# A hybrid encoder on one core: rotary tables built in three parts, and new step times in a list scheduler

## The chip, the cores and the metric

The kernel runs on one core of a Trainium2 chip. The metric is the device time of one execution in microseconds, the median of several runs. TensorE (PE in the profile, PEld for its weight loads) does the matmuls and transposes, VectorE (DVE) and ScalarE (ACT) the elementwise work, GpSimd (POOL) part of the weight preparation, one convolution channel block and the rotations, SyncE (SP) issues most of the transfers.

## The reference

Two layers over 512 tokens of width 1024. Each layer has three parts, and each part ends in a layer normalization of 1.414 times the residual plus the part's result.

```python
def layer(x, mem, cos, sin):
    proj = x @ w_in + b_in                       # 256 + 256 + 32 + 2 * 512 columns
    c_q, c_kv, k_r, u = split(proj)
    y_att = mla_group(c_q, c_kv, k_r, cos, sin)  # 8 heads, rms norms, rotary, softmax
    a, g = split(u)
    h = causal_conv31(a * sigmoid(g)) + dw_b     # depthwise, 512 channels
    y_conv = silu(layer_norm(h))
    x = LN1(ALPHA * x + concat(y_att, y_conv) @ w_o)
    x = LN2(ALPHA * x + memory_cross_attention(x, mem))  # 4 heads, 256 memory tokens
    x = LN3(ALPHA * x + (silu(x @ w_g) * (x @ w_up)) @ w_down)
    return x

cos, sin = cos(positions * inv_freq), sin(positions * inv_freq)   # 512 x 16 each
```

All of it is float32. The kernel keeps float32 accuracy on TensorE by splitting each operand into a rounded part and a rest, so that each product is three matmuls (`mm3`, L250 to L252).

## The kernel before, in words

**Weights.** A weight block is fetched into one of three `raw` buffers by SyncE's queue (L266). ScalarE writes its rounded part (`whi`, L314, or L312 with a gain), and GpSimd (L322) or VectorE (L318) the rest (`wlo`). The raw buffer is free for the next fetch when the rest is written.

**The start.** x comes in four tiles of 128 tokens. TensorE transposes each (`transpose_x`, L426), ScalarE writes the rounded part `xTh` (L429), VectorE the rest `xTl` (L432). The projection's blocks 0 to 2 begin on the first 256 tokens between these transposes. All of it is recorded under `issue_order`, which keeps on each engine the order in which it was written.

**The rotary tables** (`rope_tables`, L347 to L404) are sine and cosine of 64 angles on each partition. The positions come by a GpSimd transfer (L349), 61 small VectorE instructions reduce the angles to a turn, in several pieces so that no accuracy is lost, and two ScalarE activations (L400, L404) take the sines. The call is the last of the start. The instructions' order to what follows, the mixer, is not fixed, and so they mix with the mixer's first instructions.

**The mixer** is written as many streams, generators that yield before each step what the step needs: engine, cost in microseconds, buffers taken and given back, events awaited and fired, a rank. `Weave.run` is a list scheduler: it keeps a clock for each engine, takes again and again the step that can start first (by rank among those that start within 0.05 us), adds its cost to its engine's clock, and lets the stream record its instructions. `issue_order` keeps what comes out. So costs (`pe`, `dve`, `act`, `pool`, `dma`, and the numbers at each yield) shape the order of five engines, and nothing else of the program.

The streams: `gates` runs the projection blocks 0 to 7 in pairs; ScalarE adds the bias to one (L655) and takes tanh of half the other (L662, table set of tanh), VectorE multiplies them into `ch` (L664): the gate products, one for each 128 channels. `convolution(m)` begins with a ScalarE instruction into a PSUM bank (L625) and adds 30 taps on VectorE (L628). For the second channel block, `conv_pool` does it with ScalarE (L613, L617) and GpSimd (L619). `latent(t)` makes the low-rank columns (L702 and around, sums at L708), `queries`, `keys`, `values` and `item_steps` are the attention: scores, maximum (L847), exponential (L852), reciprocal (L855), division (L858), transposes (L863), mixing. `memory_kv` fetches the 256 memory tokens (L544), transposes them (L549), and makes keys and values of the cross-attention. `conv_out` transposes the convolution's result (L911), normalizes and transposes back (L925). `output_half` is the first half of the output projection.

Behind each mixer follow its second half and LN1 (`tail`), the cross-attention and the feed-forward part. They are written out by hand and have no costs.

Of the kernel before, what the change touches and what calls it, by code (L numbers as in the profile page):

```python
# [10 lines left out]
I32 = mybir.dt.int32  # L11
# [6 lines left out]
P = 128  # L18
# [3 lines left out]
NT = SEQ // P  # L22
# [110 lines left out]
def step(eng, cost, get=(), put=(), wait=(), fire=None, lag=0.0, rank=None):  # L133
    return eng, cost, get, put, wait, fire, lag, rank


def pe(n, width, m=P, **kw):
    return step("PE", n * max(width * 0.4219, 0.833 * m) * 1e-3, **kw)


def dve(width, n=1, fixed=70, **kw):
    return step("DVE", n * (width * 1.0417 + fixed) * 1e-3, **kw)


def act(width, n=1, fixed=150, **kw):
    return step("ACT", n * (width * 0.833 + fixed) * 1e-3, **kw)
# [29 lines left out]
def encoder(ctx: ExitStack, tc: tile.TileContext, x_in, mem_in, pos_in, wu, wc, wuq, wukv, wo,  # L176
            xq, xk, xv, xo, fin, fdn, vec, row, out):
    nc = tc.nc

    const = ctx.enter_context(tc.tile_pool(name="const", bufs=1))  # L180
# [146 lines left out]


    ident = const.tile([P, P], F32, name="ident")
    make_identity(nc, ident)  # L330
# [16 lines left out]
    def rope_tables():  # L347
        posi = const.tile([P, NT], I32, name="posi")
        nc.gpsimd.dma_start(out=posi, in_=pos_in)  # L349
        posf = const.tile([P, NT], F32, name="posf")  # L350
# [4 lines left out]
        def t64():  # L355
            return work[:, next(used), :]
# [13 lines left out]
        def whole(dst, src):  # L370
            nc.vector.tensor_copy(n, src)
            nc.vector.tensor_copy(m, n)
            nc.vector.tensor_tensor(dst, src, m, op=ALU.subtract)
# [3 lines left out]
        for src, i in ((al, 4), (ahf, 4), (al, 3), (al, 2), (ahf, 3)):  # L377
            nc.vector.scalar_tensor_tensor(out=tiny, in0=src, scalar=TURN_PARTS[i], in1=tiny,
                                           op0=ALU.mult, op1=ALU.add)
        tot = t64()  # L380
        for first, (src, i) in enumerate(((ahf, 0), (al, 0), (ahf, 1), (al, 1), (ahf, 2))):
            nc.vector.tensor_scalar(pr, src, TURN_PARTS[i], None, op0=ALU.mult)
            if first == 0:
                whole(tot, pr)
            else:
                whole(pr, pr)
                nc.vector.tensor_tensor(tot, tot, pr, op=ALU.add)
                whole(tot, tot)
# [14 lines left out]
        nc.vector.tensor_scalar(a2, a2, 0.25, None, op0=ALU.add)  # L403
        nc.scalar.activation(cosT.rearrange("p t f -> p (t f)"), a2, AF.Sin, scale=TWO_PI)  # L404


# [182 lines left out]
    def mixer(l, xT, blocks, x_src):  # L589
# [100 lines left out]
        def latent(t):  # L690
# [14 lines left out]
            for half in range(2):  # L705
                cs = blk(half, 272)
                yield dve(272, put=("ps",))
                nc.vector.tensor_tensor(c[:, cs], o[half][:, :272], cbias[:, cs], op=ALU.add)  # L708
            yield act(256, 2, get=("scr",), put=("scr",))
            ss = sm(2, "ss")  # L710
# [122 lines left out]
        def item_steps(n_item, pair, t, hs):  # L833
            nk = (t + 1) * P
# [8 lines left out]
            for i, par in enumerate(hs):  # L843
# [4 lines left out]
                                    op=ALU.max, negate=True)  # L848
            yield act(nk, n, put=("ps",))
            p = scr(name="p")  # L850
            for i in range(n):
                nc.scalar.activation(p[:, blk(i, nk)], sp[:, blk(i, nk)], AF.Exp, bias=mx[:, i:i + 1],  # L852
                                     accum_out=su[:, i:i + 1])
            yield dve(1)
            nc.vector.reciprocal(ri[:, :n], su[:, :n])  # L855
            yield step("DVE", n * (nk * 0.52 + 70) * 1e-3)
            for i in range(n):
# [279 lines left out]
    xT = new_xT()  # L1137
    with issue_order(tc, ORDERED):
        for t in range(2):
            transpose_x(x[t], t, xT)  # L1140
        blocks[0].first(xT)
        blocks[1].load()
        transpose_x(x[2], 2, xT)
        blocks[1].first(xT)
        blocks[2].load()
        transpose_x(x[3], 3, xT)
        blocks[2].first(xT)
        rope_tables()
    for l in range(DEPTH):
# [74 lines left out]
```

## Time and profile before

| | |
|---|---|
| median of 3 runs | 1494.85 us (1491.54 to 1496.07) |
| the profiled execution | 1493.32 us, span 1491.4 us |
| granted TensorE clock, mean | 0.994 |
| busy share: PE, PEld, DVE, ACT, POOL | 97%, 84%, 47%, 48%, 31% |
| chain that ended last | PE 75%, DVE 12%, ACT 5%, DMA 4%, POOL 3% |
| read from device memory | 213 MB |

A row of the timeline gives the start, the length, the engine, the line, what it writes and reads, and in brackets how long the engine had been idle before it and what released it. Matmuls overlap, and a row's length holds the drain at its end, so the cost of one in a row of many is the distance of two starts.

### The profile page before, as it was taken

Reading aid. Unit: us, or ns where it says so; the run is one execution under the profiler, and the core shown is the slowest. Engines: PE = TensorE matmul, PEld = TensorE weight load, DVE = VectorE, ACT = ScalarE, POOL = GpSimd, SP = SyncE. Lnnn points to the kernel's source line nnn. Section 1 sums busy time; section 2 is a strip of 40 time slices with the busy share of each in tenths; the row PEclk is TensorE's granted clock in tenths of the full one; section 3 lists DMA queues with packets and bytes.
Section 4 is the critical chain, followed back from the end, with each engine's and each line's share of the span. In section 5 each row is a group of like instructions: output and inputs, shape, how many; then the busy total and the mean of one; then the engine's idle time right before and its main releaser. Section 6 shows DMA issues by size and latency. Waiting matters only on the chain.

```text
span 1491.4 us, 21169 instructions
## 1 busy us (share of the span) xinstructions
PE 1453.1 (97%) x8152; PEld 1256.3 (84%) x8152; DVE 707.6 (47%) x1187; ACT 721.8 (48%) x1278; POOL 466.8 (31%) x665
## 2 busy tenths in 40 slices
PE   8799999999999999999999999999999999999997
PEld 7699988987988888888889999888889888888886
DVE  6999677665511111220469886685663111114005
ACT  3667773453544444553146777624525444446430
POOL 2679771000311111111148877410012111111111
PEclk9899999999999999999999999999999999999999
DMA  5325444242598888998433444423419888889871
GB/s 179 127 70 171 114 128 156 78 161 73 141 223 193 193 196 192 221 201 193 118 116 122 130 127 127 156 71 100 156 48 236 196 190 194 194 193 219 196 140 57
DMA packets 64452, 227.27 MB, mean 152 GB/s; under 512 B 7328, under 2 KB 7360, under 8 KB 64352
## 3 DMA queue, kind: packets, MB, share of 16 engines
q1 hardware_dynamic: 43616, 150.75, 31.1%
q0 software_dynamic: 20736, 75.17, 27.8%
q8 instruction: 64, 1.05, 0.3%
q14 instruction: 36, 0.29, 0.1%
HBM read 213.31 MB, written 8.39 MB: 149 GB/s over the span
## 4 chain that ended last, share of the span: by engine, by line
PE 75%; DVE 12%; ACT 5%; DMA 4%; POOL 3%; issue 1%; SPq 0%; POOLq 0%; DVEq 0%; ACTq 0%
PE accb L250 18%; PE accb L251 18%; PE accb L252 18%; PE psb L250 5%; PE psb L251 5%; PE psb L252 5%; DVE convb L628 3%; DMA raw<-in_xo 3%; DVE wlo L226 1%; DVE p L858 1%; DMA raw<-in_xq 1%; ACT whi L225 1%; PE convb L250 1%; PE convb L252 1%; PE convb L251 1%
## 5 line engine op out<-in xcount | busy, mean ns | idle before, releaser
L250 PE MATMUL accb<-xTh,whi 128*128 128x512 f32 (+1 forms) x1104 | 400.6, 365 | 1.5 <-ACT whi L225 1.3
L251 PE MATMUL accb<-xTl,whi 128*128 128x512 f32 (+1 forms) x1104 | 401.0, 364 | 0.5 <-DVE xTl L432 0.5
L252 PE MATMUL accb<-xTh,wlo 128*128 128x512 f32 (+1 forms) x1104 | 400.3, 363 | 0.1
L287 ACT CAST whi<-raw 128x1024 fp32r<-128x1024 f32 x126 | 132.7, 1055 | 339.4 <-PE accb L251 255.6
L250 PEld LDWEIGHTS accb<-xTh,whi 128*128 128x128 f32 x1104 | 208.7, 190 | 35.7 <-ACT xTh L429 2.7
L251 PEld LDWEIGHTS accb<-xTl,whi 128*128 128x128 f32 x1104 | 209.9, 190 | 32.9 <-DVE xTl L432 1.7
L252 PEld LDWEIGHTS accb<-xTh,wlo 128*128 128x128 f32 x1104 | 209.7, 190 | 32.5 <-DVE wlo L226 0.4
L289 POOL DMA_DIRECT2D wlo<-in_fin x82 | 71.0, 866 | 345.9 <-ACT wlo L288 336.6
L322 POOL TENSOR_TENSOR wlo<-raw,whi 128x1024 fp32r<-128x1024 f32 (+1 forms) x63 | 152.3, 2420 | 62.1 <-ACT whi L314 61.9
L1098 DVE SCALAR_TENSOR_TENSOR scr<-scr,accb 128x512 f32<-128x512 f32 x44 | 30.3, 688 | 253.4 <-ACT scr L1097 253.4
L628 DVE SCALAR_TENSOR_TENSOR convb<-ch,hvec,convb 128x511 f32<-128x511 f32 (+9 forms) x180 | 132.3, 735 | 5.2 <-ACT convb L625 1.7
L288 ACT ACTIVATE wlo<-whi 128x1024 fp32r<-128x1024 f32 x126 | 133.2, 1057 | 2.2
L226 DVE TENSOR_TENSOR wlo<-raw,whi 128x1024 fp32r<-128x1024 f32 (+1 forms) x49 | 56.5, 1158 | 127.2 <-ACT whi L225 126.4
L446 POOL TENSOR_SCALAR ve<-mv 128x1 f32<-128x1 f32 x32 | 27.5, 859 | 244.5 <-DVE mv L467 235.4
L289 POOL DMA_DIRECT2D wlo<-in_fdn x44 | 38.0, 863 | 198.4 <-ACT wlo L288 193.1
L1100 DVE SCALAR_TENSOR_TENSOR hid<-scr,accb 128x512 f32<-128x512 f32 x44 | 30.2, 687 | 136.7 <-PE accb L252 136.7
L225 ACT CAST whi<-raw 128x1024 fp32r<-128x1024 f32 (+1 forms) x49 | 48.9, 1002 | 84.9 <-PE accb L252 33.3
L619 POOL TENSOR_TENSOR cs<-cs,scr 128x511 f32<-128x511 f32 (+29 forms) x60 | 71.5, 1191 | 35.7 <-ACT scr L617 34.5
L314 ACT CAST whi<-raw 128x1024 fp32r<-128x1024 f32 (+1 forms) x63 | 66.7, 1060 | 4.6 <-PE accb L252 1.7
L250 PE MATMUL accb<-whi,hs 128*128 128x512 f32 x176 | 68.6, 390 | 0.0
L251 PE MATMUL accb<-wlo,hs 128*128 128x512 f32 x176 | 68.5, 389 | 0.0
L252 PE MATMUL accb<-whi,hs 128*128 128x512 f32 x176 | 68.5, 389 | 0.0
(295 smaller groups left out, 3165.8 us busy)
## 6 DMA issues: line engine op xcount, KB each, us to landing
raw<-in_fin SPq DMA_DIRECT2D x88, 512.0 KB, 3.6
wlo<-in_fin POOLq DMA_DIRECT2D x82, 512.0 KB, 5.6
raw<-in_fdn SPq DMA_DIRECT2D x44, 512.0 KB, 4.1
wlo<-in_fdn POOLq DMA_DIRECT2D x44, 512.0 KB, 5.9
raw<-in_xk SPq DMA_DIRECT2D x16, 512.0 KB, 3.6
raw<-in_xv SPq DMA_DIRECT2D x16, 512.0 KB, 3.6
raw<-in_wo SPq DMA_DIRECT2D x16, 512.0 KB, 3.6
raw<-in_xq SPq DMA_DIRECT2D x16, 512.0 KB, 3.6
```

Of the source, the lines that this page charges most:

```text
L225: nc.scalar.copy(hi, src)
L226: nc.vector.tensor_tensor(lo, src, hi.bitcast(F32), op=ALU.subtract)
L250: nc.tensor.matmul(o, l[0], r[0], start=first, stop=False)
L251: nc.tensor.matmul(o, l[0], r[1], start=False, stop=False)
L252: nc.tensor.matmul(o, l[1], r[0], start=False, stop=last)
L287: nc.scalar.copy(hi[:, :1024], raw[:, :1024])
L288: nc.scalar.activation(lo[:, :1024], hi[:, :1024].bitcast(F32), AF.Copy, scale=-1.0)
L289: nc.gpsimd.dma_start(out=lo[:, :1024], in_=src, accum_op=ALU.add)
L314: nc.scalar.copy(hi, raw)
L322: eng.tensor_tensor(lo, raw, hi.bitcast(F32), op=ALU.subtract)
L619: nc.gpsimd.tensor_tensor(o[:, d:], o[:, d:], part, op=ALU.add)
L628: nc.vector.scalar_tensor_tensor(out=o[:, d:], in0=src[:, :SEQ - d], scalar=tap(m, d), in1=o[:, d:], op0=ALU.mult, op1=ALU.add)
```

## The change

The positions are fetched at the very start, in front of the identity. `rope_tables` becomes a generator with three stops: part one (up to the small remainder, 13 VectorE instructions) is recorded behind the load of weight block 1, part two (4 instructions) behind that of block 2, part three (the rest, 44 instructions and the two sines) at the end as before. Seven transposes of the identity are recorded in front of everything on TensorE; their result is not read, and since they take a PSUM buffer, the buffers of the next transposes shift by one. And the scheduler's costs change: a matmul costs 0.4167 ns for each column and 0.105 ns for each stationary column, the squares of the rms norm 50 ns more each, an exponential 100 ns more, a reciprocal 120 ns more, and the division counts 1.04 ns instead of 0.52 for each element.

```diff
 def pe(n, width, m=P, **kw):
-    return step("PE", n * max(width * 0.4219, 0.833 * m) * 1e-3, **kw)
+    return step("PE", n * max(width * 0.4167 + 0.105 * m, 0.85 * m) * 1e-3, **kw)
...
+    posi = const.tile([P, NT], I32, name="posi")
+    nc.gpsimd.dma_start(out=posi, in_=pos_in)
     ident = const.tile([P, P], F32, name="ident")
     make_identity(nc, ident)
...
     def rope_tables():
-        posi = const.tile([P, NT], I32, name="posi")
-        nc.gpsimd.dma_start(out=posi, in_=pos_in)
+
         posf = const.tile([P, NT], F32, name="posf")
...
             nc.vector.scalar_tensor_tensor(out=tiny, in0=src, scalar=TURN_PARTS[i], in1=tiny,
                                            op0=ALU.mult, op1=ALU.add)
+        yield
         tot = t64()
...
             if first == 0:
                 whole(tot, pr)
+                yield
...
         nc.scalar.activation(cosT.rearrange("p t f -> p (t f)"), a2, AF.Sin, scale=TWO_PI)
+        yield
...
-            yield act(256, 2, get=("scr",), put=("scr",))
+            yield act(256, 2, fixed=200, get=("scr",), put=("scr",))
...
-            yield act(nk, n, put=("ps",))
+            yield act(nk, n, fixed=250, put=("ps",))
...
-            yield dve(1)
+            yield dve(1, fixed=190)
             nc.vector.reciprocal(ri[:, :n], su[:, :n])
-            yield step("DVE", n * (nk * 0.52 + 70) * 1e-3)
+            yield dve(nk, n, fixed=70)
...
     with issue_order(tc, ORDERED):
+        started = psb()
+        for _ in range(7):
+            nc.tensor.transpose(started[:, 0:P], ident, ident)
         for t in range(2):
             transpose_x(x[t], t, xT)
         blocks[0].first(xT)
         blocks[1].load()
+        rope = rope_tables()
+        next(rope)
         transpose_x(x[2], 2, xT)
         blocks[1].first(xT)
         blocks[2].load()
+        next(rope)
         transpose_x(x[3], 3, xT)
         blocks[2].first(xT)
-        rope_tables()
+        next(rope)
```

What it does to the order is shown at three places. Lines of the changed kernel are four higher in the mixer (L436 is the `xTl` of L432, L632 the tap of L628). First VectorE in the start, from the rest of weight blocks 0 and 1 on; `ropew` is the rotary tables' working tile. Before:

```order
L226 TENSOR_TENSOR wlo<-raw,whi 128x512 x4
L432 TENSOR_TENSOR xTl<-psb,xTh 128x2x128 x4
L226 TENSOR_TENSOR wlo<-raw,whi 128x512 x2
L432 TENSOR_TENSOR xTl<-psb,xTh 128x2x128 x2
L432 TENSOR_TENSOR xTl<-convb,xTh 128x2x128 x2
L351 CAST posf<-posi 128x4
```

Now, from the last instructions of part one on:

```order
L379 SCALAR_TENSOR_TENSOR ropew<-ah,ropew 128x64
L436 TENSOR_TENSOR xTl<-psb,xTh 128x2x128 x4
L226 TENSOR_TENSOR wlo<-raw,whi 128x512 x2
L384 TENSOR_SCALAR ropew<-ah 128x64
L372 CAST ropew<-ropew 128x64
L373 CAST ropew<-ropew 128x64
L374 TENSOR_TENSOR ropew<-ropew 128x64
L436 TENSOR_TENSOR xTl<-convb,xTh 128x2x128 x2
L436 TENSOR_TENSOR xTl<-psb,xTh 128x2x128 x2
L384 TENSOR_SCALAR ropew<-ropew 128x64
```

Thirteen rotary instructions now stand before the third tile's `xTl`, four before the last tile's; behind these the first gate product has 38 in front of it, where all 40 stood in one row before.

The second place is ScalarE from the start of the first convolution to the fifth weight cast of the mixer. Before:

```order
L625 ACTIVATE convb<-ch,vec,hvec 128x512
L655 ACTIVATE scr<-accb,vec 128x512
L314 CAST whi<-raw 128x1024 x2
L662 ACTIVATE scr<-accb,hvec 128x512
L613 ACTIVATE cs_406<-ch,vec,hvec 128x512
L617 ACTIVATE scr<-ch,hvec 128x511
L400 ACT_TABLE_LOAD
L400 ACTIVATE sinT<-ropew 128x64
L314 CAST whi<-raw 128x1024
```

Now:

```order
L629 ACTIVATE convb<-ch,vec,hvec 128x512
L403 ACT_TABLE_LOAD
L403 ACTIVATE sinT<-ropew 128x64
L407 ACTIVATE cosT<-ropew 128x64
L659 ACTIVATE scr<-accb,vec 128x512
L314 CAST whi<-raw 128x1024 x2
L666 ACT_TABLE_LOAD
L666 ACTIVATE scr<-accb,hvec 128x512
L617 ACTIVATE cs_414<-ch,vec,hvec 128x512
L314 CAST whi<-raw 128x1024
```

Both sines and both table loads moved in front of the second tanh, and nothing but the pooled convolution's start is left between it and the cast. In VectorE's order the second gate product stood behind nine taps with rotary instructions between them, and now stands behind ten taps with none between.

The third place is GpSimd in the second layer, up to the last tap of its convolution (128x482) and what comes behind it. Before:

```order
L619 TENSOR_TENSOR cs_7251<-cs_7251,scr 128x485
L322 TENSOR_TENSOR wlo<-raw,whi 128x1024
L805 TENSOR_TENSOR qra<-qs,cosT 128x2x16 x2
L805 TENSOR_TENSOR qrb<-qs,sinT 128x2x16 x2
L808 TENSOR_TENSOR qs<-qra,qrb 128x2x16
L809 TENSOR_TENSOR qs<-qra,qrb 128x2x16
L322 TENSOR_TENSOR wlo<-raw,whi 128x1024
L619 TENSOR_TENSOR cs_7251<-cs_7251,scr 128x484
L619 TENSOR_TENSOR cs_7251<-cs_7251,scr 128x483
L322 TENSOR_TENSOR wlo<-raw,whi 128x1024
L793 COPY qs<-maskp 128x64
L619 TENSOR_TENSOR cs_7251<-cs_7251,scr 128x482
```

Now:

```order
L623 TENSOR_TENSOR cs_7259<-cs_7259,scr 128x485
L322 TENSOR_TENSOR wlo<-raw,whi 128x1024
L623 TENSOR_TENSOR cs_7259<-cs_7259,scr 128x484
L623 TENSOR_TENSOR cs_7259<-cs_7259,scr 128x483
L623 TENSOR_TENSOR cs_7259<-cs_7259,scr 128x482
L797 COPY qs<-maskp 128x64
L809 TENSOR_TENSOR qra<-qs,cosT 128x2x16 x2
L809 TENSOR_TENSOR qrb<-qs,sinT 128x2x16 x2
```

Three weight subtractions and two query rotations that stood before the last tap stand behind it. On TensorE the transposes of the convolution's result moved with it, in front of some 140 matmuls, 96 of them of the memory keys.

## Rows read from the trace of the kernel before

**Rows 1.** The page, busy us and share of each engine

```profile
PE 1453.1 (97%) x8152; PEld 1256.3 (84%) x8152; DVE 707.6 (47%) x1187; ACT 721.8 (48%) x1278; POOL 466.8 (31%) x665
```

**Rows 2.** Stretches of the mixers: length, busy PE, PEld, DVE, ACT, POOL, clock, DMA

```profile
65.00:228.00 163.00, 157.39 (x1265) 147.11 (x1264) 133.76 (x241) 120.75 (x298) 125.87 (x202) 1.00 0.42 128
745.00:975.00 230.00, 223.66 (x1652) 204.59 (x1651) 179.79 (x314) 149.45 (x351) 155.67 (x223) 0.99 0.39 126
```

**Rows 3.** TensorE's wait for the memory tokens: timeline, and a stretch at half clock

```profile
60.65 1.11 PE L549 MATMUL psb<-ident,mem 128*128 128x128 f32 x4 [8.93 <-DMA mem<-in_mem]
...
54.30:64.60 10.30, 3.95 (x12) 3.28 (x13) 9.98 (x12) 7.60 (x11) 9.94 (x7) 0.50 0.50 167
```

**Rows 4.** Timeline of SyncE's queue, 41 to 57 us

```profile
41.52 14.44 SPq L266 DMA_DIRECT2D raw<-in_wc  x3
56.01 0.43 SPq L544 DMA_DIRECT2D mem<-in_mem  x1
```

**Rows 5.** Timeline of GpSimd, the weight subtraction at 53 us

```profile
53.26 2.35 POOL L322 TENSOR_TENSOR wlo<-raw,whi 128x1024 fp32r<-128x1024 f32 x1 [1.21 <-ACT whi L314]
```

**Rows 6.** Timeline of ScalarE, 49 to 60 us

```profile
49.25 0.82 ACT L613 ACTIVATE cs<-ch,vec,hvec 128x512 f32<-128x512 f32 x1 [8.70 <-DVE ch L664]
...
52.16 1.03 ACT L314 CAST whi<-raw 128x1024 fp32r<-128x1024 f32 x1
...
57.46 1.08 ACT L314 CAST whi<-raw 128x1088 fp32r<-128x1088 f32 x1
58.56 1.28 ACT L662 ACT_TABLE_LOAD   x1
59.85 0.69 ACT L662 ACTIVATE scr<-accb,hvec 128x512 f32<-128x512 f32 x1
```

**Rows 7.** Timeline of VectorE, 17 to 63 us

```profile
17.67 1.42 DVE L432 TENSOR_TENSOR xTl<-psb,xTh 128x256 fp32r<-128x256 f32 x4 [3.09 <-ACT xTh L429]
...
21.41 0.76 DVE L432 TENSOR_TENSOR xTl<-psb,xTh 128x256 fp32r<-128x256 f32 x2 [1.13 <-ACT xTh L429]
...
22.75 0.16 DVE L351 CAST posf<-posi 128x4 f32<-128x4 int32 x1
...
26.41 0.20 DVE L382 TENSOR_SCALAR ropew<-ropew 128x64 f32<-128x64 f32 x1
...
28.68 2.42 DVE L372 CAST ropew<-ropew 128x64 f32<-128x64 int32 x1
...
35.97 0.68 DVE L664 SCALAR_TENSOR_TENSOR ch<-scr 128x512 f32<-128x512 f32 x1
...
48.53 0.68 DVE L664 SCALAR_TENSOR_TENSOR ch<-scr 128x512 f32<-128x512 f32 x1
...
53.45 2.20 DVE L403 TENSOR_SCALAR ropew<-ropew 128x64 f32<-128x64 f32 x1
55.58 7.67 DVE L628 SCALAR_TENSOR_TENSOR convb<-ch,hvec,convb 128x498 f32<-128x498 f32 x10
```

**Rows 8.** Timeline of TensorE at the start

```profile
7.80 1.12 PE L426 MATMUL convb<-ident,x 128*128 128x128 f32 x4 [1.11 <-DMA x<-in_x]
```

**Rows 9.** Waits of TensorE in layer 1: timeline, and waits from 80 to 230 us

```profile
77.16 0.66 PE L549 MATMUL psb<-ident,mem 128*128 128x128 f32 x4 [1.13 <-DVE mTl L243]
...
PE psb L863 <- DVE p L858: 2.3, 5, 0.9
```

**Rows 10.** Layer 2: waits of TensorE, last tap of GpSimd, first transpose of the convolution

```profile
PE psb L863 <- DVE p L858: 2.5, 4, 1.0
...
905.36 1.04 POOL L619 TENSOR_TENSOR cs<-cs,scr 128x482 f32<-128x482 f32 x1 [1.16 <-ACT scr L617]
...
909.44 0.29 PE L911 MATMUL psb<-ident,ch 128*128 128x128 f32 x1
```

**Rows 11.** Timeline of TensorE, two matmuls of 256 columns

```profile
24.69 0.28 PE L251 MATMUL accb<-xTl,whi 128*128 128x256 f32 x1
24.81 0.29 PE L252 MATMUL accb<-xTh,wlo 128*128 128x256 f32 x1
```

## The prediction

> **What bounds the kernel now.** I read the page first, then the stretches of the stages, then the waits and the timeline of each engine in the one stretch where TensorE stands still. On the page TensorE is busy for 1453.1 us, 97% of the span, so only its idle time, its half-clock time and its order can give anything back [rows 1]. The profiled execution took 1493.32 us, 1.5 us less than the median of 1494.85; the sums below are made against 1493.3. In the two mixers TensorE is busy 157.4 of 163 us and 223.7 of 230 us [rows 2], so some 12 us of idle time lie there, in many small pieces; the diff reaches nothing behind the mixers.
>
> One piece is large. TensorE stops after the first half of projection block 6 at about 51.7 us and waits 8.93 us for the memory tokens, till 60.65; its clock falls to the lower level, 1.2 GHz, at about 54.3 and is back at 64.6, so that about 4 us of work run at half speed, another 2 us lost [rows 3].
>
> Why are the memory tokens late? Their transfer is issued only at 56.01, behind three weight transfers that had held SyncE's queue since 41.52 [rows 4]; it lands 4.6 us later. The last of the three needs a raw buffer, which comes free when GpSimd's subtraction that began at 53.26 ends, 2.35 us on [rows 5]. That subtraction follows ScalarE's cast at 52.16, which stood behind the start of the pooled convolution at 49.25, which had waited 8.70 us for VectorE's gate product [rows 6]. VectorE made that product only at 48.53: the first product came at 35.97 behind 40 rotary instructions, and between the two stand nine taps and most of the remaining rotary chain [rows 7]. Rotary instructions of 64 columns take 2.2 to 2.4 us instead of 0.2 (28.68, 53.45) where GpSimd subtracts at the same time (from 53.26 on) [rows 5, 7]. A chain of 0.2 us instructions on VectorE sets when TensorE gets its memory tokens.
>
> **The change, part by part.** *Rotary tables, parts one and two.* Thirteen and four instructions, 3.66 us from 22.75 to 26.41, move in front of the two waits of VectorE that end at 17.67 (3.09 us idle) and 21.41 (1.13 us idle) [rows 7]: 2.7 us fit into the first, 0.9 into the second. Cost nothing; without that cover they would delay the casts of x by at most the same 3.7 us.
>
> *Part three and the first product.* The order now puts 38 rotary instructions before the first product instead of the 23 that were left: 15 more of 0.23 us (ten in 26.41 to 28.68 [rows 7]), 3.4 us. The two long ones among them remain. First product: 35.97 - 3.66 + 3.4 = 35.7. Nothing gained yet.
>
> *The second product.* Behind the first now come 0.6 us of product, the six last rotary instructions (1.3 us) and ten taps, 7.67 us for ten [rows 7], with no rotary work between them: 35.7 + 0.6 + 1.3 + 7.7 = 45.3, not 48.53. ScalarE must have the gate's tanh by then. Its order now has, after the first product, convolution start (0.8), table load (1.28), two sines (0.5), the gate's bias step (0.7), two casts (2.0), table load (1.28), tanh (0.7), load and cast by their rows [rows 6]: from 36.4, 7.2 us, 43.6. That is 1.7 us early. Here a rule speaks against the change, since both loads now stand in front of the second product. The trace shows a load beginning 0.02 us after the cast before it (57.46 + 1.08) and the tanh 0.01 us after its end [rows 6], so nothing beside 1.28. The Trainium skill (ScalarE: Activation LUTs, "What ACT_TABLE_LOAD costs") puts a drain of 1.38 us beside each load. By that, the two drains would make the tanh end at 46.4, the memory term below 1.1 us smaller and the sum 1486.2; this case's trace does not show the drain, and I go by the row.
>
> *The memory transfer.* Between second product and cast there now stand only the product and the pooled start: 1.4 us, where 3.63 us stood with the load and sine. Cast at 46.7 instead of 52.16: 5.4 us earlier. Subtraction, last weight transfer and memory transfer follow at the same distances: issue at 50.6, landing at 55.2. TensorE's order up to that point is the same. **Gain 5.4 us.** Bounds: 0, if something else holds the transfer; 8.9 plus 2.0, the wait and the half clock. The idle time left, 51.7 to 55.2, is longer than the 2.6 us after which the clock fell, so I leave the 2 us where they are.
>
> *Warm-up transposes and the earlier table of positions.* Seven transposes of the identity, 0.28 us each at the start (1.12 us for four [rows 8]), 2.0 us, run before x arrives or in the 1.11 us wait for x at 7.80. GpSimd issues the positions' transfer first, which puts the identity 0.8 us later. A sooner clock or a later start of up to 3 us ends in the wait at 51.7 us. Nothing.
>
> *VectorE's lead in layer 1.* The four rotary instructions stretched under GpSimd from 39 to 55.6 us (the last: 2.20 instead of 0.2 [rows 7]) go, and 3.7 us went into idle time, so VectorE is some 10 us ahead. The wait for it at 77.16, 1.13 us, should go, and of the softmax waits of layer 1, 2.3 us [rows 9], about half, since the scheduler now counts 0.1 us more for an exponential, 0.12 for a reciprocal and 0.27 for a division over 512. **Gain 2.2 us**, bounds 0 and 3.4; a new order may also cost as much as these waits amount to.
>
> *The new order in layer 2.* No rotary work is there; only step times move things. A 512-column matmul counts 0.227 instead of 0.216 us, which tells the scheduler that VectorE, ScalarE and GpSimd have more time for each of TensorE's steps. Half of the softmax waits there, 2.5 us [rows 10], against somewhat tighter convolution ends (next part): **gain 0.6 us**, bounds -5 and 5 (2.5 with further small ones and the half clock behind one of them).
>
> Sum: 5.4 + 2.2 + 0.6 = 8.2; 1493.3 - 8.2 = **1485.1 us**, 0.55% below. The median may stand up to 1.5 us higher.
>
> **The rivals.** *The convolutions' transposes come too early (slower).* In layer 2 the transposes of the convolution's output begin at 909.44 [rows 10]. Some 140 matmuls that stood in front of them now stand behind: 96 of 256 columns, 11.5 us at 0.12 us from start to start [rows 11], and small ones, about 15 us in all. GpSimd's last tap ended at 906.40, 3.0 us before they began [rows 10]. On GpSimd three weight subtractions of 2.4 us and two rotations, some 2 us each, moved behind that last tap, 11 us. If GpSimd keeps its pace, the last tap ends near 895, and TensorE arrives near 894: a wait of a microsecond. But that tap had itself waited 1.16 us for ScalarE. If ScalarE sets the pace instead and the tap stays at 906, the wait is 12 us plus 2 us of half clock, and in layer 1, where the same transposes moved up by 5.5 us, some 6 more: 1493.3 - 8.2 + 20 = 1505. It decides above 13 us of such waits together. Against it: the scheduler saw ScalarE's steps too, and about a dozen of ScalarE's instructions moved behind the tap as well. Chance 0.09.
>
> *The memory wait stays.* If the tanh, not the taps, is last, or the transfer is held by another buffer, the chain gains under 2 us and the rest is the scatter of a new order: 1491. For it: all of the 5.4 us rests on one chain of six waits. Chance 0.19.
>
> *The wait shrinks below what drops the clock.* If TensorE comes later to the wait and the tokens earlier, both by a microsecond, the 2 us of half clock go, and with both layers' softmax waits at their bounds the time is 1479. Chance 0.12.
>
> **How the numbers follow.** The main case has 0.60, with its own range 1481 to 1490. Range over the cases: 1478 to 1494, which leaves out the slower rival and the lowest corner of the third. About 0.3%, 4.5 us, is what a measurement of this kernel can tell from no change; against 1494.85 faster means under 1490.4 and slower above 1499.3. Faster: 0.12 and most of the main case, 0.56, makes 0.68. Same: 0.19 plus the main case's edge, 0.23. Slower: 0.09.
>
> **What would show it.** Right: the second gate product near 45 us, its ScalarE successor and the weight cast near 47, the memory transfer issued near 50.6, TensorE's wait 3 to 4.5 us instead of 8.9; no VectorE instruction of 64 columns at 2 us after 38 us; no wait at the second pair of memory transposes. Wrong: a wait of 8 us or more there still; ScalarE's tanh ending after the tenth tap; a wait above 2 us before the convolution transposes of either layer, with GpSimd's last tap as its releaser; a stretch of half clock in the mixers longer than before.

## The result, and the profile after

The changed kernel takes 1513.07 us (median of 5 runs, 1511.20 to 1514.83), the kernel before 1491.54 us in the same comparison (5 runs, 1488.17 to 1496.07): a ratio of 1.0143, 95% interval 1.0122 to 1.0165. That is slower by 1.4%, where 0.55% faster was forecast, and outside the range.

The page of the changed kernel, span and busy times, against [rows 1]:

```profile
span 1511.1 us, 21192 instructions
PE 1460.3 (97%) x8159; PEld 1261.0 (83%) x8159; DVE 702.5 (46%) x1187; ACT 722.3 (48%) x1278; POOL 469.0 (31%) x665
```

The span grew by 19.7 us, and TensorE's busy time by 7.2 us although it does only seven transposes more, about 2 us [rows 8]: part of its work ran at half clock (a stretch of it is shown below); the rest of the 7.2 us was not taken apart. I cut the span at two kinds of TensorE's rows: the transposes of the rotated keys, `kx`, in the mixer (one row a layer) and the last matmul of the output projection's second half (`psb<-whi,yc`).

The timeline of the kernel before, TensorE, `kx` and last `yc` of layers 1 and 2:

```profile
108.61 0.60 PE L748 MATMUL psb<-ident,kx 128*128 128x128 f32 x4
...
266.57 0.39 PE L252 MATMUL psb<-whi,yc 128*128 128x512 f32 x1
...
837.86 0.60 PE L748 MATMUL psb<-ident,kx 128*128 128x128 f32 x4
...
998.14 0.39 PE L252 MATMUL psb<-whi,yc 128*128 128x512 f32 x1
```

The same of the changed kernel:

```profile
103.05 0.60 PE L752 MATMUL psb<-ident,kx 128*128 128x128 f32 x4
...
271.71 0.39 PE L252 MATMUL psb<-whi,yc 128*128 128x512 f32 x1
...
846.14 0.60 PE L752 MATMUL psb<-ident,kx 128*128 128x128 f32 x4
...
1018.77 0.39 PE L252 MATMUL psb<-whi,yc 128*128 128x512 f32 x1
```

Up to the first `kx` the change is 5.6 us ahead. From `kx` to the last `yc` layer 1 takes 168.7 us for 158.0 (266.6 to 108.6 before), layer 2 172.6 for 160.3 (837.9 to 998.1 before); between the two it loses another 3.1 us, at the start of layer 2, where TensorE's waits for GpSimd and VectorE add up to 3.4 us for 0.6 before; and behind layer 2's mixer it gains 1.0. So -5.6 + 10.7 + 3.1 + 12.3 - 1.0 = 19.5 of the 19.7 us. **The start gained about what was forecast; the two mixers lost 26 us, where my worst bounds for a new order were 5 us in layer 2 and 3.4 us in layer 1.**

Where in the mixers? Busy time by stretch (length, PE, PEld, DVE, ACT, POOL, clock, DMA), two stretches that hold most of the two mixers. Before:

```profile
95.00:280.00 185.00, 180.73 (x1362) 164.96 (x1361) 145.07 (x262) 120.35 (x298) 116.52 (x187) 1.00 0.41 126
840.00:1030.00 190.00, 184.12 (x1361) 166.84 (x1360) 141.05 (x249) 112.18 (x272) 99.23 (x148) 0.99 0.40 126
```

The changed kernel, with a short stretch at half clock:

```profile
95.00:280.00 185.00, 173.72 (x1279) 157.32 (x1278) 134.75 (x246) 113.00 (x282) 110.48 (x176) 0.98 0.40 124
840.00:1030.00 190.00, 174.79 (x1288) 157.67 (x1287) 134.53 (x238) 110.66 (x275) 107.81 (x172) 0.99 0.39 122
...
186.90:193.00 6.10, 6.03 (x27) 5.99 (x28) 3.25 (x7) 3.74 (x12) 5.38 (x13) 0.51 0.24 61
```

TensorE stands 16.3 us longer in these 375 us, and no other engine is busier in layer 1 (in layer 2 only GpSimd is, 107.8 of 190 us for 99.2), so no engine became the bound: all of them wait more for each other. In the short stretch behind the longest wait the granted clock is 0.51, that is the lower of its two levels, 1.2 GHz, and TensorE runs 27 matmuls; in the kernel before the same 6.1 us, with another mix of matmuls at full clock, hold 53.

The waits of TensorE in the changed kernel from 95 to 280 us and from 840 to 1030 us (total, times, longest), the larger rows:

```profile
PE accb L816 <- POOL qs L813: 3.8, 2, 2.9
PE psb L867 <- DVE p L862: 2.3, 3, 1.3
PE accb L250 <- DVE qTl L245: 1.6, 1, 1.6
...
PE psb L867 <- DVE p L862: 3.5, 5, 1.0
PE accb L251 <- DVE pl L243: 3.5, 4, 2.1
PE accb L250 <- ACT st L586: 1.9, 2, 1.7
```

All rows of these two answers add up to 25.8 us, the same answers of before to 9.6. The added 16 us have eight or more releasers on three engines; no single wait is it. The longest one, 2.94 us, shows how such a wait can come about; the others were not followed. Timelines of ScalarE, GpSimd and TensorE of the changed kernel, 174 to 187 us:

```profile
174.26 0.46 ACT L934 ACTIVATE scr<-psb,hvec 128x128 f32<-128x128 f32 x1 [0.66 <-PE psb L929]
...
180.09 0.56 ACT L936 ACTIVATE scr<-psb,hvec 128x128 f32<-128x128 f32 x1
180.43 1.15 ACT L314 CAST whi<-raw 128x1024 fp32r<-128x1024 f32 x1
...
181.65 2.38 POOL L322 TENSOR_TENSOR wlo<-raw,whi 128x1024 fp32r<-128x1024 f32 x1 [5.43 <-ACT whi L314]
...
184.59 1.70 POOL L809 TENSOR_TENSOR qrb<-qs,sinT 128x32 f32<-128x32 f32 x2
...
186.58 0.33 POOL L813 TENSOR_TENSOR qs<-qra,qrb 128x32 f32<-128x32 f32 x1
...
186.97 0.69 PE L816 MATMUL accb<-ident,qs 128*128 128x128 f32 x2 [2.94 <-POOL qs L813]
```

The new order puts two tiles of the convolution's output one behind the other. Their 16 activations stand on ScalarE 0.35 us apart, where the scheduler counts 0.257; the weight cast behind them comes at 180.43, GpSimd has been idle for 5.43 us, does the subtraction and only then the rotation for which TensorE has been waiting. By these two figures the 16 activations take 1.4 us more than the scheduler counts, so their cost alone is not the whole of the wait.

### The profile page after: what moved, and what is told of

Same layout as the page of the kernel before. It is cut to its first block, busy times and chain, and to the rows that moved or that the text cites. A ratio compares the mean times of both kernels' runs of the same rounds, so it can differ in the third digit from the quotient of the medians.

```text
span 1511.1 us, 21192 instructions
## 1 busy us (share of the span) xinstructions
PE 1460.3 (97%) x8159; PEld 1261.0 (83%) x8159; DVE 702.5 (46%) x1187; ACT 722.3 (48%) x1278; POOL 469.0 (31%) x665
## 4 chain that ended last, share of the span: by engine, by line
PE 73%; DVE 10%; ACT 6%; DMA 5%; issue 3%; POOL 3%; SPq 0%; POOLq 0%; DVEq 0%; ACTq 0%
PE accb L250 18%; PE accb L251 18%; PE accb L252 18%; PE psb L252 5%; PE psb L250 5%; PE psb L251 5%; DVE convb L632 3%; DMA raw<-in_xo 3%; POOL wlo L322 1%; DVE wlo L226 1%; DVE p L862 1%; PE convb L250 1%; ACT whi L225 1%; PE convb L251 1%; PE convb L252 1%
## 5 line engine op out<-in xcount | busy, mean ns | idle before, releaser
L632 DVE SCALAR_TENSOR_TENSOR convb<-ch,hvec,convb 128x511 f32<-128x511 f32 (+9 forms) x180 | 132.6, 737 | 11.0 <-ACT convb L629 6.6
```

Source lines behind the costliest of these rows:

```text
L632: nc.vector.scalar_tensor_tensor(out=o[:, d:], in0=src[:, :SEQ - d], scalar=tap(m, d), in1=o[:, d:], op0=ALU.mult, op1=ALU.add)
```

## The experiments

Eighteen kernels, each against the kernel before on the same chip; the kernel before had medians of 1490.3 to 1491.5 us, so the medians of the table can be compared with each other to about a microsecond. "Stretches" are `kx` to last `yc` in layers 1 and 2 (158.0 and 160.3 before, 168.7 and 172.6 after).

| kernel | median us | ratio, 95% | stretches |
|---|---|---|---|
| tables_only | 1483.29 | 0.9947 [0.9930, 0.9964] | 157.7, 159.0 |
| pe_cost_only | 1510.69 | 1.0136 [1.0117, 1.0155] | 171.0, 162.1 |
| soft_cost_only | 1501.38 | 1.0071 [1.0056, 1.0086] | 168.1, 160.5 |
| costs_only | 1518.70 | 1.0188 [1.0171, 1.0205] | 169.0, 172.5 |
| pe_up_half | 1499.79 | 1.0061 [1.0044, 1.0078] | 167.8, 162.1 |
| pe_down_half | 1497.91 | 1.0056 [1.0039, 1.0073] | 163.7, 164.5 |
| hop_up | 1500.53 | 1.0063 [1.0046, 1.0080] | 167.8, 168.4 |
| pe_down_7 | 1501.94 | 1.0079 [1.0064, 1.0094] | 169.8, 168.5 |
| all_up_8 | 1501.58 | 1.0077 [1.0062, 1.0092] | 165.1, 169.2 |
| after_hop | 1511.53 | 1.0149 [1.0133, 1.0164] | 166.6, 172.9 |
| after_pe_down | 1508.93 | 1.0140 [1.0120, 1.0160] | 178.9, 160.8 |
| calib_act | 1509.79 | 1.0122 [1.0107, 1.0137] | 169.2, 165.1 |
| calibrated | 1493.76 | 1.0022 [1.0011, 1.0032] | 156.8, 169.2 |
| calib_hop | 1488.15 | 0.9988 [0.9977, 1.0000] | 163.9, 160.4 |
| calib_pe_down | 1490.34 | 1.0002 [0.9993, 1.0012] | 167.3, 160.5 |
| no_warmup | 1484.60 | 0.9960 [0.9946, 0.9975] | 158.1, 158.9 |
| mem_early | 1484.12 | 0.9959 [0.9944, 0.9974] | 157.8, 159.1 |
| mem_both_early | 1484.99 | 0.9955 [0.9939, 0.9972] | 157.7, 159.3 |

**The two halves of the change.** *tables_only* is the changed kernel with the old step times, *costs_only* the kernel before with the new ones; *pe_cost_only* and *soft_cost_only* put in one part of these.

```diff
 # costs_only = both hunks, pe_cost_only = the first, soft_cost_only = the others
-    return step("PE", n * max(width * 0.4219, 0.833 * m) * 1e-3, **kw)
+    return step("PE", n * max(width * 0.4167 + 0.105 * m, 0.85 * m) * 1e-3, **kw)
...
+            yield act(256, 2, fixed=200, get=("scr",), put=("scr",))
...
+            yield act(nk, n, fixed=250, put=("ps",))
...
+            yield dve(1, fixed=190)
...
+            yield dve(nk, n, fixed=70)
```

> The rotary tables in three parts and the warm-up transposes, with all step times of the scheduler as before. If the loss comes from the step times (both theories below), the 6 us that the memory wait gave back stay: 1484 to 1487 us, ratio 0.995 to 0.997. Rival: the three parts cost something behind the memory wait as well; then 1493 us or more.

> The kernel before, with the new cost of a matmul alone. Theory R (ratio): TensorE's cost was too low by about the share by which those of the other engines are too low; raised alone it makes the scheduler count on VectorE, ScalarE and GpSimd being done sooner than they are. Then this edit alone carries the loss: 1508 to 1520 us. Theory S (softmax): the longer softmax steps move the transposes and with them the fill work; then this one stays within 4 us of 1491.5.

> The kernel before, with the new costs of squares, exponentials, reciprocals and divisions alone. Theory R: within 4 us of 1491.5, or somewhat faster, since these costs give the other engines more room. Theory S: it carries the loss, 1508 to 1520 us.

> The kernel before, with all new step times and none of the other edits. If the edits add up, the changed kernel's 1513 plus the 6 us of the memory wait: 1517 to 1521 us under R and S alike. If the tables' new place is part of the loss, under 1510 us.

The tables gain 7.2 us (1490.5 to 1483.3, just below the range expected). The step times lose 28.2 us alone. Their sum, 21.0, is close to the measured 21.5. The order says the same: counted in the traces (tiles by name, buffer numbers left out), TensorE's order of *tables_only* is that of the kernel before, and that of *costs_only* is that of the changed kernel, but for the seven transposes and 16 places, all in the first 21 us. Each part of the step times loses by itself, the matmuls' 20 us, in theory R's range, and the softmax's 11 us, which neither theory had. Whether that is due to these numbers or to any other numbers, these runs do not tell; the next group asks it. Undoing the step times and keeping the tables gives the fastest kernel of this study (with *no_warmup* and the two *mem* kernels, which lie within 1.7 us of it).

**Neighbours of the old step times.** Do the new numbers lose, or would any numbers? In *tables_only* the matmul's number goes up or down by half a per cent or down by 7%, or the price of a hand-over between engines goes from 0.15 to 0.16 us; *all_up_8* takes the new matmul numbers and multiplies the steps of the other three engines by 1.08.

```diff
-    return step("PE", n * max(width * 0.4219, 0.833 * m) * 1e-3, **kw)
+    return step("PE", n * max(width * 0.4240, 0.837 * m) * 1e-3, **kw)   # pe_up_half
+    return step("PE", n * max(width * 0.4198, 0.829 * m) * 1e-3, **kw)   # pe_down_half
+    return step("PE", n * max(width * 0.3924, 0.775 * m) * 1e-3, **kw)   # pe_down_7
...
-    HOP = 0.15
+    HOP = 0.16                                                           # hop_up
...
-    return step("DVE", n * (width * 1.0417 + fixed) * 1e-3, **kw)
+    return step("DVE", n * (width * 1.0417 + fixed) * 1.08e-3, **kw)     # all_up_8; ACT, POOL alike
```

> The tables-only kernel (1483.3 us), with a matmul's cost raised by 0.5% and nothing else. Theory R (what counts is TensorE's cost against that of the other engines): half a percent is a tenth of the new cost's 5 to 11%, so within 2 us: 1481 to 1486. Theory N (any other numbers give another order, and the order before was a chosen one): 5 us or more above, 1488 to 1505 us, since half of the order changes already.

> The tables-only kernel, with a matmul's cost lowered by 0.5%. Theory R: within 2 us of 1483.3, or slightly faster. Theory N: 1488 to 1505 us, as for the raise.

> The tables-only kernel, with a matmul's cost lowered by 7%, the new cost's step in the other direction. Theory R: the other engines get more room; 1475 to 1486 us, not slower. Theory N: 1488 to 1505 us.

> The tables-only kernel, with the new cost of a matmul and 8% more on every step of VectorE, ScalarE and GpSimd, so that the ratio between the engines is the old one. Theory R: the loss of the new matmul cost (20 us) goes: 1480 to 1488 us. Theory N: another order, 1488 to 1508 us, no better than the new matmul cost alone beyond chance.

> The rotary tables alone, with the scheduler's price of a hand-over between engines 0.16 instead of 0.15 us and all step times as they were. No engine's ratio to another changes. Theory N (the old order is a good one among many, and any other number breaks it): 1488 to 1505 us. Theory that it is the step times of particular engines that matter: at most 1486 us.

Five times 1498 to 1502, theory N's range each time; the other theory's ranges, none of them above 1488, were missed each time. Half a per cent on one number, in either direction, puts another instruction in 1,777 or 1,975 of TensorE's 8,159 places, all in the two mixers, and costs 15 to 17 us; the new step times do so in 1,921. So the old order, 1483.3 with the tables, is far better than what its own numbers give next door, and the usual price of leaving it is some 16 us of the 30 that the new step times cost. By this measure the softmax's 11 us is no more than any other numbers cost, and the matmuls' 20 us little more. The two largest of TensorE's waits of *hop_up* from 95 to 280 us:

```profile
PE accb L251 <- DVE pl L243: 3.6, 3, 1.7
PE psb L867 <- DVE p L862: 2.7, 4, 1.1
```

*all_up_8* shows the same from the other side: with all engines' steps raised, the loss is 11 us smaller than the changed kernel's, and no smaller than a neighbour's. *pe_down_7*, the step in the other direction, is no better than a neighbour either. In *hop_up* the waits are again many, here almost all on VectorE: 20.5 us in both stretches, against 9.5 in *tables_only*.

**Neighbours of the new step times, and a full set.** *calibrated* is the changed kernel with the other engines' steps set to the distances in its trace too; *calib_act* sets ScalarE's alone. *after_hop*, *after_pe_down*, *calib_hop* and *calib_pe_down* are neighbours of the two.

```diff
-def act(width, n=1, fixed=150, **kw):
+def act(width, n=1, fixed=190, **kw):                     # calibrated, calib_act
...
-            yield act(P, 8, put=("ps",))
+            yield act(P, 8, fixed=238, put=("ps",))       # calibrated, calib_act
...
-            yield dve(u.n, **kw) if u.vector else pool(u.n * 2.25e-3, **kw)
+            yield dve(u.n, **kw) if u.vector else pool(u.n * 2.33e-3, **kw)
...
-                yield dve(SEQ - d, fixed=130, lag=1.0 if d == TAPS - 1 else 0.13)
+                yield dve(SEQ - d, fixed=235, lag=1.0 if d == TAPS - 1 else 0.03)
...
-            yield pool(1.3)
+            yield pool(1.57)
```

> The changed kernel, with the other engines' step times also set to the distances in its trace: ScalarE's fixed part 190 ns for 150, the convolution's output activations 238, the taps 235 with a lag of 0.03, a rotary step on GpSimd 1.57 us, the low part of a weight 2.33 ns per column. Theory C (the loss is that only some engines were set, so that the queue of ScalarE and GpSimd is planned too short): at most 1485 us. Theory N (closer numbers pick just another order): 1490 to 1508 us.

> The changed kernel with the price of a hand-over 0.16 instead of 0.15 us. Theory D (every set of numbers draws one order out of the same lot, and 1513 and 1483 are draws from its two ends): 1493 to 1506 us, like the neighbours of the old numbers (1498 to 1501). Theory C (the new set is worse on average, since matmuls were raised to the trace and the queues of ScalarE and GpSimd were not): 1508 to 1520 us.

> The changed kernel with its new step times of matmuls 0.5% lower (0.4146, 0.1045 and 0.846 for 0.4167, 0.105 and 0.85). Theory D: 1493 to 1506 us. Theory C: 1508 to 1520 us.

> The calibrated kernel (1493.8 us) with the price of a hand-over 0.16 instead of 0.15 us. Theory D: 1493 to 1506 us, mean near 1500, since 1493.8 is a draw too. Theory C (with all engines set to the trace the orders are better on average): 1486 to 1496 us.

> The calibrated kernel (1493.8 us) with its step times of matmuls 0.5% lower. Theory D: 1493 to 1506 us, mean near 1500. Theory C: 1486 to 1496 us.

> The changed kernel with only ScalarE's step times set to its trace (fixed part 190 ns for 150, the convolution's output activations 238), GpSimd and the taps as they were. Theory A (the late weight halves and rotations behind the long ScalarE queue are the loss): 1486 to 1498 us, as with all engines set. Theory G (GpSimd's and VectorE's short steps are the larger part): 1503 to 1514 us.

The neighbours of the changed kernel fell into theory C's range, those of *calibrated* too; *calibrated* by itself fell into theory N's, and *calib_act* into theory G's. Three orders from each set do not overlap: 1508.9, 1511.5 and 1513.1 with the new step times, 1497.9 to 1500.5 for the neighbours of the old, 1488.2, 1490.3 and 1493.8 with all engines set. Their means are 1511.2, 1499.4 and 1490.7: on these orders, correcting only the matmuls and the softmax costs about 12 us against the old numbers' neighbours, and correcting the rest as well gains about 9. Two things weaken this. The old set is counted without its own order, 1483.3, which is better than every order of the full set, while the other two sets are counted with theirs. And the three of a set are not independent draws: *calib_hop* and *calib_pe_down* differ in only 217 of TensorE's 8,159 places, so that the full set stands on two orders, and *after_hop* differs from the changed kernel in 1,232. That the numbers matter on the average of many orders is likely by this, and not shown. With ScalarE alone set, 1509.8, nothing comes back beyond the scatter of the changed kernel's neighbours: what is missing lies in GpSimd's and VectorE's steps or needs all three. They were not tried apart. TensorE's waits of *calib_hop* from 840 to 1030 us add up to 4.5 us, against 15.0 in the changed kernel; from 95 to 280 us they add up to 7.5 against 10.8, and more than half is the wait for a rotation on GpSimd that was followed above, 3.6 us at its longest. So that kind of wait is not what the full set took away. The largest of the later stretch and of the earlier one:

```profile
PE psb L867 <- DVE p L862: 1.3, 2, 1.0
...
PE accb L816 <- POOL qs L813: 4.6, 3, 3.6
```

**The start.** *no_warmup* is *tables_only* without the seven transposes; *mem_early* fetches the first block of memory tokens in the start, *mem_both_early* both; `memory_kv` then takes these blocks in place of its own fetch (that edit is left out below). The order of TensorE, VectorE, ScalarE and GpSimd stays the same in the two.

```diff
-        started = psb()                                   # no_warmup
-        for _ in range(7):
-            nc.tensor.transpose(started[:, 0:P], ident, ident)
...
         blocks[2].first(xT)
+        for m in range(2):                                # range(1) in mem_early
+            early.append(bigt([P, D], F32, name="mem"))
+            nc.sync.dma_start(out=early[m], in_=mem_in[blk(m), :])
         next(rope)
```

> The rotary tables alone (the run before that gave 1483.3 us), without the seven warm-up transposes; the order of the rest is the same on every engine. Theory that they cost and give nothing, since TensorE waits for the first tokens either way: 1481 to 1486 us. Theory that the granted clock in the start depends on them: at least 2 us slower than 1483.3, with a lower clock in the first 25 us.

> The rotary tables alone, with the first block of memory tokens fetched in the start, ahead of the weights of the up projection; the order on TensorE, VectorE, ScalarE and GpSimd stays the same, one DMA moves forward on SP's queue. The wait for the memory tokens (4.4 us left) and the half-speed clock behind it should go: about 1477 us, 1475 to 1480. Rival: the weights behind it come later by the time of its bytes and TensorE waits there instead: 1482 to 1487 us.

> The rotary tables alone (1483.3 us), with both blocks of memory tokens fetched in the start, the order of TensorE, VectorE, ScalarE and GpSimd as it was. With only the first block early, the wait for the first (5.1 us) went and one for the second (4.8 us) took its place. Theory that the fetch alone held it: both waits and the half clock behind them go, 1477 to 1481 us. Rival: the weights fetched behind them come late and the wait moves once more: 1482 to 1486 us.

The warm-up is worth nothing that these runs can tell: 1484.6 against 1483.3, with ranges that overlap. Nor does it hold the clock up: over the first 25 us the granted clock is 0.93 in *tables_only*, and 1.00 without the seven transposes and in *mem_both_early*, which has them. Fetching the tokens early gains nothing either (1484.1 and 1485.0, each in its rival's range). *tables_only*, timelines of SyncE and TensorE:

```profile
50.48 0.43 SPq L548 DMA_DIRECT2D mem<-in_mem  x1
...
55.22 1.11 PE L553 MATMUL psb<-ident,mem 128*128 128x128 f32 x4 [5.14 <-DMA mem<-in_mem]
```

*mem_early*, timeline of TensorE, first and third group of these transposes:

```profile
51.00 0.60 PE L558 MATMUL psb<-ident,mem 128*128 128x128 f32 x4
...
66.64 1.08 PE L558 MATMUL psb<-ident,mem 128*128 128x128 f32 x4 [4.84 <-DMA mem<-in_mem]
```

The wait for the first block is gone and one of 4.84 us for the second has come in its place. *mem_both_early*, timeline of TensorE, and busy time from 50 to 80 us:

```profile
64.33 0.39 PE L251 MATMUL psb<-wlo,xTh 128*128 128x272 f32 x1 [2.25 <-POOL wlo L322]
69.31 1.11 PE L558 MATMUL psb<-ident,mem 128*128 128x128 f32 x4 [3.33 <-DVE mTl L243]
...
50.00:80.00 30.00, 23.93 (x144) 21.73 (x143) 27.54 (x37) 17.87 (x31) 23.66 (x22) 0.89 0.41 134
```

No transfer is waited for there now, and TensorE stands as long: 2.25 us for GpSimd's weight rest and 3.33 us for VectorE. VectorE is busy for 27.5 of these 30 us, and GpSimd had worked without a pause from 49.3 us on when it ended that rest at 64.3. The transfer was only the last in line; behind it stand VectorE and GpSimd. That their work sets how soon TensorE can pass this place is what these rows say; no run took work from either of them.

## Why the prediction was wrong, point by point

*Right: the memory transfer.* These rows of the changed kernel's timeline, and a stretch around the wait, answer to [rows 3 to 7]:

```profile
34.91 0.68 DVE L668 SCALAR_TENSOR_TENSOR ch<-scr 128x512 f32<-128x512 f32 x1
...
44.45 0.69 DVE L668 SCALAR_TENSOR_TENSOR ch<-scr 128x512 f32<-128x512 f32 x1
...
40.62 1.28 ACT L666 ACT_TABLE_LOAD   x1
41.91 0.69 ACT L666 ACTIVATE scr<-accb,hvec 128x512 f32<-128x512 f32 x1
45.17 0.82 ACT L617 ACTIVATE cs<-ch,vec,hvec 128x512 f32<-128x512 f32 x1 [2.57 <-DVE ch L668]
45.90 1.03 ACT L314 CAST whi<-raw 128x1024 fp32r<-128x1024 f32 x1
...
49.82 0.43 SPq L548 DMA_DIRECT2D mem<-in_mem  x1
...
54.65 1.11 PE L553 MATMUL psb<-ident,mem 128*128 128x128 f32 x4 [4.39 <-DMA mem<-in_mem]
...
48.30:59.00 10.70, 6.30 (x22) 4.88 (x21) 10.28 (x15) 7.02 (x9) 10.70 (x7) 0.71 0.56 181
```

First gate product 34.9 for 35.7 forecast, second 44.45 for 45.3, cast 45.9 for 46.7, issue 49.8 for 50.6, landing 54.65 for 55.2: a gain of 6.0 us for 5.4. The lead of 0.8 us is there from the first product on, and the distances along the chain are the forecast's to within 0.3 us. TensorE came to the wait at 50.3 us and not at 51.7, so it still stood 4.39 us. The tanh was done at 42.6, before the taps were, as I had it, and its load again began right behind the cast and was followed by the tanh at 0.01 us. The drain of 1.38 us that the Trainium skill (ScalarE: Activation LUTs, "What ACT_TABLE_LOAD costs") puts beside a load does not show in this trace. By that rule the sum was 1486.2; its extra 1.1 us would have come from a later tanh, and the tanh was not late. The half clock stayed, as forecast (granted clock 0.71 over the stretch from 48.3 to 59.0 us). It fell some 2.6 us into the wait here too; in *tables_only* it was still 1.00 up to 55.0 us, 4.9 us into a wait of 5.14, so the 2.6 us of the forecast are what one wait showed, and no rule. What I did not see is that VectorE's and GpSimd's work stands right behind the transfer, so that an earlier transfer did not bring the gain near its upper bound of 10.9 (*mem_both_early*).

*Right: rotary parts one and two, and the warm-up, at nothing.* In the changed kernel the `xTl` behind part one begins at 17.10 us and the first behind part two at 20.46, where they began at 17.67 and 21.41; *no_warmup* shows the other.

*Half right: VectorE's lead in layer 1 (2.2 us).* The wait of 1.13 us for `mTl`, the rest of the memory tokens, shrank to 0.36 [rows 9]. The softmax waits did not: 2.3 us before, 2.1 with the tables alone, 2.3 in the changed kernel. With the old step times the tables gave 6.7 us of span, which is what they had given by the first `kx` (101.8 for 108.6).

***The step that failed: "The new order in layer 2: gain 0.6 us", bounds -5 and 5.*** Layer 2 lost 12.3 us from `kx` on and some 3 before it. In layer 1 the same step had no term but a clause ("a new order may also cost as much as these waits amount to", 3.4 us); there it lost 10.7. I took the sizes of the waits in the order before as the measure of what a new order could cost, and read the new step times as a correction: nearer to the trace, so rather better. The first was wrong: with other numbers the list scheduler gave another order through both mixers, and five such orders, half a per cent away or further, cost 15 to 19 us each where my bounds were 5 and 3.4. I had no row that could bound them. The second is not borne out: the correction was one-sided, since a 512-column matmul counts 0.227 instead of 0.216 us, which tells the planner that the others have 5% more time for each of TensorE's steps, while ScalarE's and GpSimd's stayed too short (0.257 us counted for an activation that takes 0.35). The prediction saw this sign ("has more time for each of TensorE's steps") and counted it as a gain. That it is what costs the changed kernel more than its neighbours rests on the three sets of orders above.

*The slower rival* had the right sign and the wrong place. The convolution's transposes did come early, at 904.59 in layer 2, but the last tap had left GpSimd at 902.7 and they did not wait for it. What came instead are the waits of the two answers above, on three engines; in the one that was followed, the convolution's output on ScalarE pushed a weight and a rotation back (the chain at 174 us). Of the signs of being wrong one came: half clock in layer 1's mixer, where the kernel before had none from 95 to 280 us.

**How far the cause is shown.** Shown: the loss is the step times' alone, 28 us without the tables and 30 with them; it lies in the mixers' order; five other sets of numbers cost 15 to 19 us against this old order, and setting all engines takes some 20 of the 30 us back. Likely, on few and related orders: that some 12 us more belong to this half-corrected set. Not borne out: that the planner counts VectorE's taps too short. A tap in a row of taps takes 0.77 us from start to start, and the planner's cost is 0.65; but the planner also holds the next tap of that convolution back by 0.13, 0.78 in all, and leaves VectorE free in between. The trace shows both numbers. Timeline of VectorE, changed kernel:

```profile
45.06 11.55 DVE L632 SCALAR_TENSOR_TENSOR convb<-ch,hvec,convb 128x501 f32<-128x501 f32 x15
56.51 0.68 DVE L668 SCALAR_TENSOR_TENSOR ch<-scr 128x512 f32<-128x512 f32 x1
...
83.55 0.73 DVE L632 SCALAR_TENSOR_TENSOR convb<-ch,hvec,convb 128x495 f32<-128x495 f32 x1
84.18 0.42 DVE L243 TENSOR_TENSOR cTl<-psb,cTh 128x256 fp32r<-128x256 f32 x1
```

Fifteen taps take 11.45 us to the next start, and a tap with another step behind it 0.63; over the run, where VectorE did not pause, 118 taps with a tap behind them take 0.774 us in the mean, and 50 with another step 0.658. So the old numbers had the taps right, and the full set, with 0.75 and 0.03, counts a single tap too long: it is not nearer to the trace in every step. Open: which of the full set's steps bring the gain, or whether its two orders are good ones by chance, and why the old numbers' order is 15 us better than its neighbours. An order that had been kept as the best of several would look just so; no run here tells.

## What to carry to other kernels

When a number of a list scheduler changes, its order can change all through, so forecast with the scatter of its neighbours, not with the waits of the order that you see; here half a per cent on one number moved the time by 15 to 17 us. Judge a set of numbers by several neighbours (another 0.5%, another hand-over price), look whether these are really different orders, and keep the best order found; here no corrected set came back to the 1483.3 us of the old numbers. Before a step's cost is corrected, read from the trace what the next instruction sees, of the same stream and of another one: the two can differ, as with the taps. And when the last releaser of a wait is removed, look at which engines are busy nearly without a pause in that stretch: here they held the next waits.

## What the runs showed of the hardware

GpSimd's instructions are also stretched beside VectorE's, not only the other way [rows 5, 7]: two instructions of a rotation, 32 columns each, took 1.70 us at 184.59 where two took 0.45 at 184.17, and between 184.90 and 186.17 VectorE ran two 512-column subtractions into `yc`. Three more such instructions, one in the changed kernel and two in the kernel before, took 0.70 us where 0.25 is usual, each beside a subtraction into `yc`. In the changed kernel's start the stretched VectorE instructions coincide with GpSimd's two subtractions one by one. Timelines of GpSimd and VectorE, 27 to 33 us, and of VectorE at 184.90:

```profile
27.14 2.40 POOL L322 TENSOR_TENSOR wlo<-raw,whi 128x1024 fp32r<-128x1024 f32 x1 [15.67 <-ACT whi L314]
30.07 2.40 POOL L322 TENSOR_TENSOR wlo<-raw,whi 128x1024 fp32r<-128x1024 f32 x1 [0.53 <-ACT whi L314]
...
27.18 2.41 DVE L384 TENSOR_SCALAR ropew<-ah 128x64 f32<-128x64 f32 x1
29.63 0.20 DVE L372 CAST ropew<-ropew 128x64 int32<-128x64 f32 x1
29.86 0.20 DVE L373 CAST ropew<-ropew 128x64 f32<-128x64 int32 x1
30.09 2.46 DVE L374 TENSOR_TENSOR ropew<-ropew 128x64 f32<-128x64 f32 x1
...
184.90 1.27 DVE L243 TENSOR_TENSOR yc<-scr,yc 128x512 fp32r<-128x512 f32 x2
```

The first of VectorE's instructions that begins after a subtraction of GpSimd ends only with it; the two that fall between the subtractions take 0.20 us.
